# The values' products of two attentions by two query blocks, in float32r parts

## The chip, the cores and the metric

The kernel runs on one core of a Trainium2 chip. The core has a matrix engine (TensorE, PE in the rows; its loading of the stationary operand is PEld), a vector engine (VectorE, DVE), an engine for functions of one operand (ScalarE, ACT), a general one (GpSimd, POOL) and one that starts transfers (SyncE, SP). Each works through its own queue in order, and waits for the others by semaphores. Products land in PSUM, which has banks of 128 x 512 float32; only VectorE and ScalarE read them out in this kernel. The metric is the time of one execution in microseconds on the device.

## The reference

Two transformer layers over 1024 tokens of 1024 features, all in float32. The change touches one attention of each. In both, a query's weights are taken with the values of the keys up to its own block of 128 queries:

```
# layer 1: stick-breaking attention, 8 heads of 64
z = einsum('bhqd,bhkd->bhqk', q, k) * scale
log_keep = where(mask, log_sigmoid(-z), 0)             # mask: key < query
rest = cumsum(log_keep, reverse=True) - log_keep
a = where(mask, exp(log_sigmoid(z) + rest), 0)
out = einsum('bhqk,bhkd->bhqd', a, v)
# layer 2: latent attention (MLA), 8 heads, keys of 96, values of 64
logits = where(allowed, einsum('bhqd,bhkd->bhqk', q, k) * scale, -1e30)
out = einsum('bhqk,bhkd->bhqd', softmax(logits), v)
```

Beside them stand a gated delta rule, projections and gates in layer 1, and a differential attention, a feed-forward block and a gated embedding in layer 2. They keep their code, but for where they lie beside the two attentions.

## The kernel before

**Parts.** Most products run on operands that are split into two float32r parts, high and low, whose sum is the float32 value: `mm3` makes three products of them (L252 to L254). Weights are split by GpSimd (`W`, L243, L244), what comes out of PSUM by `split_evac`: ScalarE casts the high part out of the bank (L301), and VectorE then subtracts it from the same bank for the low part (L302). The products of weights and values (L907) are the exception: they are plain float32, and such a product is two records in the trace.

**The two attentions.** `sb` (L855 to L878) and `mla` (L1171 to L1220) go through the heads in four pairs, and for each pair through eight query blocks of 128. Blocks 0 to 3 take both heads in one item, blocks 4 to 7 one head per item: 12 items a pair. `s0` makes an item's logits `z` in PSUM (two buffers of two banks) and its weights `e` (in `sb` ScalarE's absolute value, exponential and logarithm, VectorE's scan, and another exponential into `cs`; in `mla` VectorE's maximum, ScalarE's exponential with its sum and GpSimd's scaling). `s1` runs two items behind (`attend`, skew 2) and calls `attend_pv`: for up to four blocks of weights at a time it transposes them on TensorE into one PSUM bank `pt` (L903), has them copied to `aT` (L904: VectorE in `sb`; in `mla` ScalarE for an item's first copy and VectorE for its second), and then multiplies (L907) with the values as the stationary operand, 64 columns wide, and 128 queries moving. One bank `po` gathers two heads of a query block, and VectorE copies it to `ob` (L878, L1220).

**Banks and filling.** `banks(2, 1)` is in force in both stages: two banks for projections (`pj`), one for transposes (`pt`), four for `z`, one for `po`. `mix` puts units of other projections between the yields of an attention: in `sb` the projections of the first layer (`proj_z` among them), in `mla` what is left of `diff_proj`, the differential attention's projection, of which the first part runs beside `mla_proj`. `diff_proj` transposes its queries and keys through the same `pt` bank, and a tile `qb_st` with two buffers goes to DRAM. A scheduler then places each engine's instructions, so that rows of all these stand mixed in the queues.

**Where the values come from.** Three places write them to DRAM, each by a ScalarE copy: `vba` (L494, layer 1's first four heads), `proj_b` (L785, `vt2`), and `k_mm` (L1096, a tile `l_v` of four token tiles, in `mla_proj`). `dr_v` and `dr_mv` hold them in float32, and each attention loads a pair's values in one transfer. In `mla_proj`, `fin` transposes queries and keys (L1124), splits them (`l_st`) and sends them off (L1127).

Of the kernel before, what the change touches and what calls it, by code (L numbers as in the profile page):

```python
# [11 lines left out]
F32 = mybir.dt.float32  # L12
# [10 lines left out]
D = 1024  # L23
# [6 lines left out]
# ---------------------------------------------------------------- host layout  # L30
# [121 lines left out]
class Kern:  # L152
    def __init__(self, ctx, tc, d, out):
        self.tc, self.nc, self.d, self.out = tc, tc.nc, d, out
        self.ctx = ctx
        self.const = ctx.enter_context(self.pool("const"))
# [21 lines left out]

    def banks(self, n, m):
        """from here on n banks for products, m for transposes"""  # L180
# [10 lines left out]
    def consts(self):  # L191
# [19 lines left out]
        # strict causal mask in [query, key] layout: key >= query masked  # L211
# [3 lines left out]
        # keys of the next 64-chunk, hidden from the first half of a query block  # L215
# [40 lines left out]
    def fm(self, w, act, kt, ct, half):  # L256
        """feature-major [128 features, 512 tokens] of weight column tile ct"""
# [6 lines left out]
    def tm(self, w, act, kt, tp, c0=0, n=256):  # L264
        """token-major [128 tokens, 2 token tiles, n features]"""
# [8 lines left out]
    def rsqrt(self, v, n, scale, eps, pool=None):  # L274
        """(v * scale + eps) ** -0.5 of a [128, n] tile, in full float32"""
# [21 lines left out]
    def split_evac(self, hi, lo, ps, scale=None):  # L297
        """hi + lo = ps * scale, both f32r"""
# [18 lines left out]
    def norm_half(self, get, gain, xn, pool, h):  # L317
        """rms norm of 4 token-major tiles, transposed to feature-major f32r pairs"""
# [21 lines left out]
    def norm_in_place(self, x, gain, pool, evac, deep=False):  # L340
        """the same of [128, 4, D] in place, and what evac does with its transposes"""
# [23 lines left out]
    def mix(self, main, fill, end=2.0):  # L365
        """units of fill between those of main; both yield how far they are, and fill is at end when main is done"""
# [7 lines left out]
    # ------------------------------------------------------------ layer 1  # L374
    def layer1(self):
# [3 lines left out]
        self.dr_v = dr("dr_v", [2, NT, 128, 256])  # L379
# [105 lines left out]
    def proj_a(self, wv, w):  # L485
# [3 lines left out]
        def vba(w, t):  # L489
# [6 lines left out]
            nc.sync.dma_start(self.dr_v[0, t], vt)  # L496

        def conv(c, u):
            """causal convolution and silu"""
# [11 lines left out]
        def post(c, s):  # L511
            """token-major keys and values, sums of squares"""
# [47 lines left out]
    def gdr(self):  # L560
# [13 lines left out]
        def chunk(c):  # L574
# [32 lines left out]
            # q and k in place times exp(cumulated decay)  # L607
# [10 lines left out]
            for l in range(5):  # L618
                # rows of the second block of each pair, columns of the first
# [65 lines left out]
            # o * rsqrt(mean(o^2) + EPS * dk * (ssq + EPS))  # L685
# [14 lines left out]
        # two chunks at a time, half a chunk apart  # L700
# [976 lines left out]
```

## Time and profile before

| | us |
|---|---|
| median of 3 runs | 2750.32 |
| lowest and highest run | 2749.12, 2760.20 |
| span of the profiled execution | 2761.4 |
| TensorE busy in it | 2628.9 (95%) |
| VectorE busy | 1454.1 (53%) |
| ScalarE busy | 865.7 (31%) |
| GpSimd busy | 1058.8 (38%) |

The profiled execution lies near the slowest of the three runs. The stick-breaking stage stands at about 558 to 940 us of the span, the latent queries', keys' and values' projection at 1180 to 1440, the latent attention at 1440 to 1650, the differential attention behind it. A duration in a row is an instruction's own, from start to end; TensorE's instructions overlap, so that the distance from one start to the next says what one costs in a stream.

### The profile page before, as it was taken

The page shows a single profiled execution, that of the slowest core. Times are in us where ns is not written, and L with a number is a line of the kernel's source. Part 1 is how long each engine was busy: PE and PEld are TensorE (multiplying, and loading weights), DVE is VectorE, ACT ScalarE, POOL GpSimd, SP SyncE. Part 2 cuts the span into 40 slices and gives each one's busy share as a digit, 9 for nine tenths or more (in the row PEclk, how much of TensorE's full clock was granted, in tenths as well). Part 3 has the DMA queues.
Part 4 walks back from the last instruction along what each step waited for, and adds up shares of the span by engine and source line. Part 5 has one row for each costly group of instructions (what it writes and reads, how often), then busy time and mean ns, then how long its engine had stood idle before and what let it go on. Part 6 is the DMA issues. An engine that isn't in the chain of part 4 may idle for free. (4 is left out here: it accounts for less than half of the span.)

```text
span 2761.4 us, 38977 instructions
## 1 busy us (share of the span) xinstructions
PE 2628.9 (95%) x15298; PEld 2201.4 (80%) x15298; DVE 1454.1 (53%) x2837; ACT 865.7 (31%) x1575; POOL 1058.8 (38%) x920
## 2 busy tenths in 40 slices
PE   6998999999999999999889999999999999999999
PEld 6888888877777778989777786779777777777789
DVE  6665555275666554457844334765544454534372
ACT  3322222153344332122324333563433333201031
POOL 2433332212122234544533231223577777633322
PEclk9999999999999999999999996999999999999999
DMA  4423223242321355322673336444212222433222
GB/s 152 136 99 108 69 85 100 74 117 82 106 68 64 111 193 182 115 78 83 207 200 119 98 121 164 136 147 167 65 63 91 78 65 89 164 110 101 75 81 89
DMA packets 150031, 307.27 MB, mean 111 GB/s; under 512 B 13876, under 2 KB 57140, under 8 KB 149848
## 3 DMA queue, kind: packets, MB, share of 16 engines
q1 hardware_dynamic: 149848, 304.78, 35.2%
q8 instruction: 121, 1.98, 0.3%
q14 instruction: 62, 0.51, 0.1%
HBM read 207.72 MB, written 99.37 MB: 111 GB/s over the span
## 5 line engine op out<-in xcount | busy, mean ns | idle before, releaser
L243 POOL TENSOR_SCALAR hl<-raw 128x512 fp32r<-128x512 f32 (+3 forms) x270 | 198.3, 739 | 968.9 <-PE pj L254 958.2
L244 POOL TENSOR_TENSOR hl<-raw,hl 128x512 fp32r<-128x512 f32 (+3 forms) x270 | 368.9, 1372 | 16.2
L252 PE MATMUL pj<-hl,xn_0h 128*128 128x256 f32 (+2 forms) x544 | 161.3, 297 | 2.4 <-DVE qb_raw L730 1.2
L253 PE MATMUL pj<-hl,xn_0h 128*128 128x256 f32 (+2 forms) x544 | 161.1, 296 | 1.7 <-POOL hl L244 1.7
L252 PE MATMUL pj<-hl,xn_1h 128*128 128x256 f32 (+2 forms) x544 | 159.4, 293 | 0.0
L254 PE MATMUL pj<-hl,xn_1l 128*128 128x256 f32 (+2 forms) x544 | 159.4, 293 | 0.0
L254 PE MATMUL pj<-hl,xn_0l 128*128 128x256 f32 (+2 forms) x544 | 159.3, 293 | 0.0
L253 PE MATMUL pj<-hl,xn_1h 128*128 128x256 f32 (+2 forms) x544 | 158.9, 292 | 0.0
L1508 POOL TENSOR_TENSOR hl<-w_s,hl 128x512 fp32r<-128x512 f32 x88 | 121.5, 1382 | 84.1 <-ACT hl L1507 84.0
L907 PE MATMUL po<-aT,v 128*64 128x128 f32 x1152 | 150.1, 280 | 0.8 <-DVE ob L1220 0.5
L252 PE MATMUL pj<-hl,f_hh 128*128 128x512 f32 x352 | 139.8, 397 | 5.0 <-DVE xres L1618 2.8
L254 PE MATMUL pj<-hl,f_hl 128*128 128x512 f32 x352 | 140.4, 401 | 2.9 <-DVE f_hl L1609 2.9
L907 PEld LDWEIGHTS po<-aT,v 128*64 128x64 f32 x1152 | 116.5, 136 | 29.3 <-issue 21.0
L253 PE MATMUL pj<-hl,f_hh 128*128 128x512 f32 x352 | 138.3, 393 | 0.0
L904 DVE COPY aT<-pt 128x512 f32<-128x512 f32 (+3 forms) x128 | 72.6, 567 | 120.2 <-PE pt L903 120.1
L1618 DVE TENSOR_TENSOR xres<-xres,pj 128x512 f32<-128x512 f32 x96 | 65.1, 685 | 127.6 <-PE pj L254 114.6
L1508 POOL TENSOR_TENSOR hl<-raw,hl 128x512 fp32r<-128x512 f32 x66 | 100.1, 1522 | 71.6 <-ACT hl L1507 70.9
L1563 DVE TENSOR_TENSOR f_u<-pj,w_u 128x512 f32<-128x512 f32 x44 | 30.4, 692 | 170.4 <-ACT w_u L1531 96.3
L252 PE MATMUL pj<-xn_0h,hl 128*128 128x512 f32 x288 | 116.9, 406 | 0.0
L252 PE MATMUL pj<-xn_1h,hl 128*128 128x512 f32 x288 | 115.9, 403 | 0.0
L254 PE MATMUL pj<-xn_0h,hl 128*128 128x512 f32 x288 | 114.8, 399 | 0.0
L254 PE MATMUL pj<-xn_1h,hl 128*128 128x512 f32 x288 | 114.6, 398 | 0.0
(599 smaller groups left out, 7505.3 us busy)
## 6 DMA issues: line engine op xcount, KB each, us to landing
raw<-in_w_o_dram SPq DMA_DIRECT2D x28, 512.0 KB, 4.3
dr_mla<-l_st SPq DMA_DIRECT2D x32, 384.0 KB, 4.0
qk<-dr_mla SPq DMA_DIRECT2D x32, 384.0 KB, 4.9
raw<-in_w_fg_dram SPq DMA_DIRECT2D x22, 512.0 KB, 4.5
raw<-in_w_fu_dram SPq DMA_DIRECT2D x22, 512.0 KB, 3.5
dr_h<-f_y SPq DMA_DIRECT2D x22, 512.0 KB, 5.3
raw<-in_w_fd_dram SPq DMA_DIRECT2D x22, 512.0 KB, 4.0
f_y<-dr_h SPq DMA_DIRECT2D x22, 512.0 KB, 4.4
```

Of the source, the lines that this page charges most:

```text
L243: nc.gpsimd.tensor_scalar(hl[:, 0], raw[:, k:k + c], 1.0, 1.0, ALU.mult, ALU.mult)
L244: nc.gpsimd.tensor_tensor(hl[:, 1], raw[:, k:k + c], hl[:, 0].bitcast(F32), ALU.subtract)
L252: mm(ps, lh[0], rh[0], start=first, stop=False)
L253: mm(ps, lh[0], rh[1], start=False, stop=False)
L254: mm(ps, lh[1], rh[0], start=False, stop=last)
L904: copy[b0 > 0](aT[:, b0:b0 + len(bs), :], pt[:, :len(bs), :])
L907: mm(po[64 * h:64 * h + 64, :], v[:, j, h * 64:h * 64 + 64], aT[:, b, :], start=j == 0, stop=j == i)
L1508: nc.gpsimd.tensor_tensor(hl[:, 1], v, hl[:, 0].bitcast(F32), ALU.subtract)
L1563: nc.vector.tensor_tensor(u, ps, v, ALU.add)
L1618: nc.vector.tensor_tensor(xr, xr, ps, ALU.add)
```

## The change

- **Values in two parts.** The three places write high and low parts by `split_evac` instead of a copy. `dr_v` and `dr_mv` double: per head 64 high columns and 64 low ones beside each other. `l_v` now holds two token tiles and is sent twice as often, with one buffer.
- **Two query blocks at a time.** `attend_two` replaces `attend` for both: when the second block of a pair of blocks `u` has its weights and the delay (skew 2 in `sb`, 1 in `mla`, counted in items) has passed, `s1` runs once for both. The new `attend_pv` goes by pairs of key blocks. For each head it transposes four blocks (three in the last pair) into the bank `pt`, and `split_evac` makes two float32r parts of them. Then come the products, for each key block, head and part one: the stationary operand is 128 columns, high and low values, the moving one 256 queries (128 for the last key block). In `po` the first 64 rows gather the high values' share, the others the low values'; `halves` adds them (ScalarE copy, VectorE addition), per head.
- **Counts.** Per attention: 320 float32r products instead of 288 float32 ones (576 records); the same 288 transposes, in 80 fillings of the bank instead of 88; 80 casts and 80 subtractions instead of 88 copies; 16 transfers of `ob` instead of 4 (`sb`) or 8 (`mla`).
- **Buffers.** `e` has 7 instead of 2 and `cs` 4 in `sb` (the scan now runs in place), and 5 instead of 3 in `mla`; `aT` has 3 and 2. `qb_st` has one buffer instead of two in layer 2. The values are loaded by halves, the second half later, and `mla` loads its queries and keys in another order.

```diff
@@ vba
-            vt = cv.tile([128, 256], F32, tag="vt", name="vt")
-            nc.scalar.copy(vt, ps[:, :256])
+            vt = cv.tile([128, 4, 2, 64], F32R, tag="vt", name="vt")
+            self.split_evac(vt[:, :, 0], vt[:, :, 1], ps[:, :256].rearrange("p (h f) -> p h f", h=4))
...
@@ qk_stack
-                st = pool.tile([128, 2, 512], F32R, tag="qb_st", name="qb_st", bufs=2)
+                st = pool.tile([128, 2, 512], F32R, tag="qb_st", name="qb_st", bufs=1 + (pool is not self.fp))
...
@@ sb
-            e = new("e", 2)
+            e = new("e", 7)
...
-            cs = new("cs", 4)
+            cs = e
...
@@ k_mm, in the loop over four token tiles
-                nc.scalar.copy(vt[:, j], pv[:, :, 1, :])
+                if j % 2 == 0:
+                    vt = lp.tile([128, 2, 4, 2, 64], F32R, tag="l_v", name="l_v", bufs=1)
+                self.split_evac(vt[:, j % 2, :, 0], vt[:, j % 2, :, 1], pv[:, :, 1, :])
...
@@ mla
-            e = sp.tile([128, 1024], F32, tag="e", name="e", bufs=3)[:, :len(hs) * nk].rearrange("p (a k) -> p a k", a=len(hs))
+            e = sp.tile([128, 1024], F32, tag="e", name="e", bufs=5)[:, :len(hs) * nk].rearrange("p (a k) -> p a k", a=len(hs))
...
-        def s1(p, i, hs):
...
+        def s1(p, u):
             qks, v = st[p]
...
+            po = po_.tile([128, 2, 256], F32, tag="po", name="po")
+            yield from self.attend_pv(sp, po, self.weights(st, p, u), v, u, 2)
+            ob = sp.tile([128, 256], F32, tag="ob", name="ob", bufs=1)
+            self.halves(ob, po)
+            nc.sync.dma_start(self.dr_mix[:, p, u * 256:(u + 1) * 256], ob)
...
+        yield from self.attend_two(s0, s1, 1)
@@ attend_pv
+        for jp in range(u + 1):
+            slots = [(j, a) for j in (2 * jp, 2 * jp + 1) for a in range(2) if j <= 2 * u + a]
+            aT = []
+            for h in range(2):
+                pt = self.PT()
+                for b, (j, a) in enumerate(slots):
+                    nc.tensor.transpose(pt[:, b, :], e[a, h][:, j * 128:j * 128 + 128], self.ident)
+                n = len(slots)
+                hl = sp.tile([128, 2, 4, 128], F32R, tag="aT", name="aT", bufs=bufs)
+                self.split_evac(hl[:, 0, :n], hl[:, 1, :n], pt[:, :n])
+                aT.append(hl)
+            for j in (2 * jp, 2 * jp + 1):
+                b = [n for n, s in enumerate(slots) if s[0] == j]
+                q = slice((2 - len(b)) * 128, 256)
+                for h in range(2):
+                    for n in range(2):
+                        nc.tensor.matmul(po[:, h, q], v[j // 4][:, j % 4, h], aT[h][:, n, b[0]:b[-1] + 1],
+                                         start=j + n + h == 0, stop=j == 2 * u + 1 and n + h == 2, skip_group_check=True)
+            yield
+    def halves(self, ob, po):
+        for h in range(2):
+            R = slice(64 * h, 64 * h + 64)
+            self.nc.scalar.copy(ob[R], po[0:64, h])
+            self.nc.vector.tensor_tensor(ob[R], ob[R], po[64:128, h], ALU.add)
```

The change also moves instructions. In the queues below `pt`, `aT`, `po`, `z` and `pj` are the tiles named above, `hl` a weight's part, `xn_1h` and `mix00h` operands of projections; what stands in brackets are the engines' semaphores that the row waits for. L936 and L946 are the changed kernel's transposes and products, L255 its third line of `mm3`, L954 `halves`.

TensorE in the stick-breaking stage before, one item's transposes and part of its products:

```order
L903 MATMUL pt<-cst,cs 128x128 [waits PE_49,Activation_49]
L903 MATMUL pt<-cst,cs 128x128 x3
L252 MATMUL pj<-xn_0h,hl 128x512 [waits Pool_49]
L253 MATMUL pj<-xn_0l,hl 128x512
L254 MATMUL pj<-xn_0h,hl 128x512 [waits Pool_49]
L252 MATMUL pj<-xn_0h,hl 128x512
L907 MATMUL po<-aT,v 64x128 [waits DVE_49]
L907 MATMUL po<-aT,v 64x128 x3
```

and in the same stage of the changed kernel, one pair of key blocks, from the second head's transposes on:

```order
L936 MATMUL pt<-cst,e 128x128 [waits DVE_49]
L936 MATMUL pt<-cst,e 128x128 x3
L946 MATMUL po<-aT,v 128x256
L255 MATMUL pj<-xn_1h,hl 128x512
L253 MATMUL pj<-xn_1h,hl 128x512
L254 MATMUL pj<-xn_1l,hl 128x512
L946 MATMUL po<-aT,v 128x256 [waits Activation_49]
L255 MATMUL pj<-xn_1h,hl 128x512
L253 MATMUL pj<-xn_1h,hl 128x512
L254 MATMUL pj<-xn_1l,hl 128x512
L255 MATMUL pj<-xn_1h,hl 128x512
L253 MATMUL pj<-xn_1h,hl 128x512
```

In both a projection's rows stand between the transposes and the products that need them; the transposes now wait for VectorE, which reads the bank second.

TensorE in the last pair of heads of the latent attention before:

```order
L903 MATMUL pt<-cst,e 128x128 [waits Activation_49]
L903 MATMUL pt<-cst,e 128x128 x2
L907 MATMUL po<-aT,v 64x128 x4
L253 MATMUL pj<-hl,mix00h 128x256
L254 MATMUL pj<-hl,mix00l 128x256
L252 MATMUL pj<-hl,mix01h 128x256
L253 MATMUL pj<-hl,mix01h 128x256
L254 MATMUL pj<-hl,mix01l 128x256
L907 MATMUL po<-aT,v 64x128 [waits DVE_49]
L907 MATMUL po<-aT,v 64x128 x2
```

and in the changed kernel, also in the latent attention behind the filling's last row:

```order
L946 MATMUL po<-aT,v 128x256 [waits DVE_49]
L946 MATMUL po<-aT,v 128x256 x4
L936 MATMUL pt<-cst,e 128x128 [waits PE_49]
L936 MATMUL pt<-cst,e 128x128 x3
L946 MATMUL po<-aT,v 128x256 [waits Activation_49]
L936 MATMUL pt<-cst,e 128x128 [waits DVE_49]
L936 MATMUL pt<-cst,e 128x128 x3
L946 MATMUL po<-aT,v 128x256
L946 MATMUL po<-aT,v 128x256 [waits Activation_49]
L946 MATMUL po<-aT,v 128x256 [waits DVE_49]
L946 MATMUL po<-aT,v 128x256 x4
```

No projection's row is left between them: transposes and products alternate, and five products stand between VectorE's subtraction and the next transposes.

ScalarE near the end of the latent attention before (L1207 the exponentials, L1235 a filling's copy):

```order
L904 COPY aT<-pt 128x512 [waits PE_49,Activation_49] x2
L1207 ACTIVATE e,a_s<-z,a_m 128x896 [waits DVE_49,Pool_49]
L904 COPY aT<-pt 128x512 [waits PE_49,Activation_49]
L1207 ACTIVATE e,a_s<-z,a_m 128x896 [waits DVE_49,Pool_49]
L1207 ACTIVATE e,a_s<-z,a_m 128x1024 [waits DVE_49,Pool_49]
```

and in the changed kernel (L1268 the exponentials, L302 the casts):

```order
L302 CAST aT<-pt 128x512 [waits DVE_49,PE_49,Activation_49]
L302 CAST aT<-pt 128x512 [waits DVE_49,PE_49]
L1268 ACTIVATE e,a_s<-z,a_m 128x896 [waits PE_49,Pool_49]
L302 CAST aT<-pt 128x384 [waits DVE_49,PE_49]
L1268 ACTIVATE e,a_s<-z,a_m 128x1024 [waits Pool_49]
L302 CAST aT<-pt 128x384 [waits DVE_49,PE_49]
L954 COPY ob<-po 64x256 [waits DMAHW2_49,PE_49]
L1268 ACTIVATE e,a_s<-z,a_m 128x1024 [waits DVE_49]
```

An exponential now stands between two casts of one group, and waits for TensorE (the transposes that free its buffer) where it waited for VectorE's maximum.

## Rows read from the trace of the kernel before

**Rows 1.** Busy time of each engine in the two attentions' stretches, with granted clock.

```profile
core 0: us, PE busy (x) PEld busy (x) DVE busy (x) ACT busy (x) POOL busy (x), PEclk, DMA share, GB/s
558.00:940.00 382.00, 380.05 (x1951) 276.33 (x1951) 238.86 (x291) 162.95 (x203) 76.96 (x72) 1.00 0.27 82
1440.00:1650.00 210.00, 207.29 (x1469) 165.72 (x1468) 84.27 (x173) 81.83 (x182) 61.12 (x77) 1.00 0.39 117
```

**Rows 2.** Groups by line and shape, 558 to 940 us: busy, mean ns, idle before.

```profile
L907 PE MATMUL po<-aT,v 128*64 128x128 f32 x572 | 74.8, 280 | 0.3 <-DVE aT L904 0.2
```

**Rows 3.** The same view of 1440 to 1650 us.

```profile
L907 PE MATMUL po<-aT,v 128*64 128x128 f32 x576 | 74.9, 280 | 0.5 <-DVE ob L1220 0.5
...
L1207 ACT ACTIVATION_READ_ACCUMULATOR e<-z,a_m 128x1 f32 x60 | 11.9, 198 | 0.0
...
L1207 ACT ACTIVATE e<-z,a_m 128x1024 f32<-128x1024 f32 x8 | 8.9, 1115 | 5.2 <-DVE a_r L1208 2.4 <-DVE a_m L1204 2.1 <-PE pt L903 0.7
```

**Rows 4.** Timeline of TensorE near 701 us: start, duration, engine, line, operation.

```profile
700.80 0.38 PE L903 MATMUL pt<-cst,cs 128*128 128x128 f32 x2
701.11 1.52 PE L907 MATMUL po<-aT,v 128*64 128x128 f32 x12
702.56 0.50 PE L254 MATMUL pj<-xn_1h,hl 128*128 128x512 f32 x1
702.90 0.39 PE L252 MATMUL pj<-xn_1h,hl 128*128 128x512 f32 x1
703.13 0.40 PE L253 MATMUL pj<-xn_1l,hl 128*128 128x512 f32 x1
```

**Rows 5.** Timeline near 1563 us, in the latent attention.

```profile
1562.76 0.59 ACT L904 COPY aT<-pt 128x512 f32<-128x512 f32 x1 [3.04 <-PE pt L903]
...
1563.39 0.44 PE L903 MATMUL pt<-cst,e 128*128 128x128 f32 x2
...
1563.87 0.42 DVE L904 COPY aT<-pt 128x256 f32<-128x256 f32 x1 [0.83 <-PE pt L903]
```

**Rows 6.** What the transposes (L903) sat idle for, us and times.

```profile
  DVE aT L904: 7.7, 21
  ACT aT L904: 7.6, 28
```

**Rows 7.** Timeline of TensorE near 1570 us.

```profile
1570.29 0.28 PE L252 MATMUL pj<-hl,xn_0h 128*128 128x256 f32 x1
1570.41 0.28 PE L253 MATMUL pj<-hl,xn_0h 128*128 128x256 f32 x1
```

**Rows 8.** Timeline near 1459 us: transposes, cast and subtraction of a query stack.

```profile
1458.21 0.63 PE L747 MATMUL pt<-cst,qb_raw 128*128 128x128 f32 x4
...
1458.88 0.58 ACT L301 CAST qb_st<-pt 128x512 fp32r<-128x512 f32 x1 [1.67 <-PE pt L747]
...
1459.49 0.69 DVE L302 TENSOR_TENSOR qb_st<-pt,qb_st 128x512 fp32r<-128x512 f32 x1
```

**Rows 9.** Busy time of the tiles pj alone (PE, PEld, DVE, ACT), the latent attention.

```profile
1440.00:1650.00 210.00, 37.23 (x253) 31.98 (x252) 0.69 (x1) 3.51 (x6) 1.00 0.39 117
```

**Rows 10.** Busy time by stretch, where the granted clock is low (columns of rows 1).

```profile
1430.00:1440.00 10.00, 6.14 (x29) 5.98 (x30) 1.45 (x4) 3.00 (x9) 1.30 (x4) 0.69 1.08 238
1680.00:1720.00 40.00, 39.72 (x118) 25.80 (x119) 18.78 (x67) 17.09 (x48) 0.00 (x0) 0.50 0.42 119
```

**Rows 11.** Timeline of TensorE, 1433 to 1436 us, the latent attention's first products.

```profile
1433.86 0.45 PE L252 MATMUL z<-qk 96*128 96x128 f32 x1 [4.74 <-DMA qk<-dr_mla]
...
1435.76 0.41 PE L253 MATMUL z<-qk 96*128 96x256 f32 x1
1435.97 0.41 PE L254 MATMUL z<-qk 96*128 96x256 f32 x1
```

**Rows 12.** Busy time in a stretch of the latent projection (columns of rows 1).

```profile
1340.00:1350.00 10.00, 9.38 (x70) 8.50 (x69) 9.87 (x42) 6.66 (x19) 1.92 (x2) 1.00 0.95 306
```

**Rows 13.** The tile l_v: from its transfer's issue to its landing.

```profile
DMA to landing us min/median/max: 2.9/4.2/4.7
```

**Rows 14.** The tile l_st: what its engines sat idle for, us and times.

```profile
  DMA dr_mla<-l_st: 28.6, 17
```

More of the change, by code (lines that the diff above doesn't have):

```diff
@@ L828, in sb, with values @@
         st = {}
+        def values(p, half):
+            v = sp.tile([128, 4, 2, 128], F32R, tag=f"v{half}", name="v", bufs=2 - half)
+            nc.sync.dma_start(v.bitcast(F32).rearrange("p t h f -> p t (h f)"), self.dr_v[p // 2, 4 * half:4 * half + 4, :, 2 * (p % 2):2 * (p % 2) + 2].rearrange("t p h a f -> p t (h a f)"))
+            st[p][1].append(v)
         def first(p):
             qk = [self.load_qk(sp, self.dr_qk[p], 0)]
-            v = sp.tile([128, NT, 128], F32, tag="v", name="v", bufs=2)
-            nc.sync.dma_start(v, self.dr_v[p // 2, :, :, (p % 2) * 128:(p % 2) * 128 + 128].rearrange("t p f -> p t f"))
+            v = []
             st[p] = [qk, v]
+            values(p, 0)
         def s0(p, i, hs):
@@ L840, in s0 @@
                 st[p][0].append(self.load_qk(sp, self.dr_qk[p], 1))
-                st[p].append(sp.tile([128, 1024], F32, tag="ob", name="ob", bufs=1))
+            if i == 2:
+                values(p, 1)
             if i == 4 and hs[0] == 0 and p < 3:
@@ L887, in pairs, with attend_two @@
         return [(p, i, hs) for p in range(4) for i in range(NT) for hs in ([(0, 1)] if i < 4 else [(0,), (1,)])]
-    def attend_pv(self, sp, po_, st, e, v, i, hs, *copy):
-        nc = self.nc
-        mm = nc.tensor.matmul
-        if hs[0] == 0:
-            st["po"] = po_.tile([128, 128], F32, tag="po", name="po")
-        po = st["po"]
-        blocks = [(a, j) for a in range(len(hs)) for j in range(i + 1)]
-        aT = sp.tile([128, 8, 128], F32, tag="aT", name="aT", bufs=2)
-        step = 4 if i != 2 else 3
-        for b0 in range(0, len(blocks), step):
-            pt = self.PT()
-            bs = blocks[b0:b0 + step]
-            for b, (a, j) in enumerate(bs):
-                nc.tensor.transpose(pt[:, b, :], e[:, a, j * 128:j * 128 + 128], self.ident)
-            copy[b0 > 0](aT[:, b0:b0 + len(bs), :], pt[:, :len(bs), :])
-        for b, (a, j) in enumerate(blocks):
-            h = hs[a]
-            mm(po[64 * h:64 * h + 64, :], v[:, j, h * 64:h * 64 + 64], aT[:, b, :], start=j == 0, stop=j == i)
-        return po
+    def attend_two(self, s0, s1, skew):
+        items = self.pairs()
+        size = lambda it: (it[1] + 1) * len(it[2]) + 6
+        total, done = sum(size(it) for it in items), 0
+        for n in range(len(items) + skew):
+            if n < len(items):
+                s0(*items[n])
+                done += size(items[n]) / 2
+                yield done / total
+            if n < skew:
+                continue
+            p, i, hs = items[n - skew]
+            if i % 2 and hs[-1] == 1:
+                u = i // 2
+                part = sum(size(it) for it in items if it[0] == p and it[1] // 2 == u) / 2 / (u + 1)
+                for _ in s1(p, u):
+                    done += part
+                    yield min(1.0, done / total)
@@ new lines, in weights, with attend_pv @@
+    def weights(self, st, p, u):
+        e = {}
+        for a in range(2):
+            i = 2 * u + a
+            for hs in [(0, 1)] if i < 4 else [(0,), (1,)]:
+                w = st.pop((p, i, hs))
+                for k, h in enumerate(hs):
+                    e[a, h] = w[:, k]
+        return e
+    def attend_pv(self, sp, po, e, v, u, bufs):
+        nc = self.nc
+        for jp in range(u + 1):
[17 more added lines that the diff above has]
+            yield
@@ L1168, in load, with values @@
         def load(p, hh, c, half):
-            t = sp.tile([96, 2, 512], F32R, tag=f"qk{c}{half}{hh}", name="qk", bufs=1 + (hh == 1 and c == 1 and half == 0))
+            if c:
+                t = sp.tile([96, 2, 512], F32R, tag=f"k{half}{hh}", name="k", bufs=1 + (hh == 1 and half == 0))
+            else:
+                t = sp.tile([96, 2, 512], F32R, tag="q", name="q", bufs=3)
             nc.sync.dma_start(t.bitcast(F32), self.dr_mla[2 * p + hh][:, 2 * c:2 * c + 2, half * 512:half * 512 + 512])
             st[p][0][hh, c, half] = t
+        def values(p, half):
+            v = sp.tile([128, 4, 2, 128], F32R, tag=f"v{half}", name="v", bufs=1)
+            nc.sync.dma_start(v.bitcast(F32).rearrange("p t h f -> p t (h f)"), self.dr_mv[:, 4 * half:4 * half + 4, 2 * p:2 * p + 2].rearrange("p t h a f -> p t (h a f)"))
+            st[p][1].append(v)
         def first(p):
-            v = sp.tile([128, NT, 128], F32, tag="v", name="v", bufs=2)
+            v = []
             st[p] = {}, v
-            for key in ((1, 1, 0), (0, 0, 0), (1, 0, 0)):
+            for key in ((1, 1, 0), (0, 0, 0)):
                 load(p, *key)
-            nc.sync.dma_start(v, self.dr_mv[:, :, p * 128:p * 128 + 128])
         def s0(p, i, hs):
@@ L1184, in s0 @@
                     first(p)
-                for key in ((0, 1, 0), (0, 1, 1), (0, 0, 1), (1, 1, 1), (1, 0, 1)):
+                for key in ((0, 1, 0), (1, 0, 0), (0, 1, 1), (0, 0, 1), (1, 1, 1)):
                     load(p, *key)
-            if i == 4 and hs[0] == 0 and p < 3:
-                first(p + 1)
+            if i == 1:
+                values(p, 0)
+            if i == 4 and hs[0] == 0:
+                load(p, 1, 0, 1)
+                values(p, 1)
+                if p < 3:
+                    first(p + 1)
             nk = (i + 1) * 128
```

43 lines of the change are left out of this document (17 added, 26 removed).

## The prediction

> **What bounds the kernel now.** I read three views in this order: the busy time by stretch, the groups of instructions by line and shape, and the timeline of single products. The change touches two stages of attention and three places where values are written, so each is read by its own stretch. In the stick-breaking stage TensorE is busy for 380.05 of 382 us and in the latent stage for 207.29 of 210, at full clock in both; VectorE has 239 and 84 us there, ScalarE 163 and 82 [rows 1]. So both stages are bounded by TensorE's own work, and the next engine has room. The values' product itself is 572 and 576 records of 74.8 and 74.9 us busy [rows 2, 3], but those durations overlap. In the timeline twelve records (six products, a float32 product being two records) go from 701.11 to 702.56: 0.121 us a record. The float32r product behind them takes 0.34 us to the next one, where the one after takes 0.23: leaving float32 costs 0.11 [rows 4].
>
> The other thing to see is the one PSUM bank for transposes. Before, a single reader empties it: a copy begins at 1562.76, lasts 0.59, and the next transposes begin at 1563.39 [rows 5]. With 0.6 of transposes ahead that is about 1.3 us for each filling. TensorE waits for that in only 7.7 + 7.6 us of the whole program [rows 6], because other products stand in its queue.
>
> **Stick-breaking stage, TensorE.** Removed: 576 records x 0.121 = 70 us, and 48 exits (one for each item of the stage, 4 pairs x 12) x 0.11 = 5. Added: 320 float32r products for 288 float32 ones, 256 of them 256 columns wide. Such a product begins 0.12 us after the one ahead of it [rows 7], 256 x 0.12 = 31. The 64 of 128 columns are not in the trace in this form; they cost no more than a 256-column one and no less than half of it, 64 x 0.06 to 0.12 = 4 to 8, and I take the lower, since a stream shrinks with its columns here (0.23 for 512, 0.12 for 256). So TensorE gets 75 - 35 = 40 us less.
>
> **The bank gets two readers.** Now ScalarE casts the high part out of the bank and VectorE subtracts from the same bank behind it, and only then may the next transposes write it. The kernel has this pattern already in another step: four transposes at 1458.21, cast at 1458.88 for 0.58, subtraction at 1459.49 for 0.69, bank free at 1460.18 [rows 8]. That is 1.97, with a signal 2.03 us a filling against 1.3. There are 80 fillings per attention instead of 88. In the order, the five products that wait for VectorE's subtraction stand ahead of the next transposes once per pair of key blocks, 5 x 0.12 = 0.6, 40 times. The chain is 80 x 2.03 + 40 x 0.6 = 186 us. In the stick-breaking stage TensorE still has 380 - 40 = 340 us, and the projection's rows stand between the transposes and the products in the order, so the chain is covered. What isn't: the casts queue behind the absolute value, exponential and logarithm on ScalarE, the subtractions behind the scan on VectorE. The nearest row is the 7.7 us by VectorE's copies [rows 6]; times 2.03 / 1.3 it is 12, 4 more; the far end is that 40 of the 80 fillings wait for the whole subtraction, 40 x 0.69 = 28. I take 7, near the row. **Term: -33 us (-44 to -12; the low end has no wait and 4 us for entries into float32 that I don't count).** The output's evacuation becomes four operations instead of two per two blocks; the next block's transposes and cast (1.25 us) run meanwhile, so I cost it at nothing; with that cover gone it is at most 0.6 + 0.69 a block, 16 blocks, 20 us.
>
> **Latent stage.** Here the filling work, another attention's projection, ends early in the new order: its last row stands in the third group of the second pair of heads, and from there some 2.4 of the 4 pairs have nothing but their own work. TensorE's own work for a pair was about 43 us (207 less the filling's 37 [rows 9], over 4) and falls by 10 to 33. The chain of a pair is 20 x 2.03 = 41, less 8 x 0.3 where a filling has three blocks (an estimate: 0.125 of transposes and some 0.1 each of cast and subtraction), plus 10 x 0.6: 44 us. Moreover the weights' five buffers come free by the last transposes of a group, so about five exponentials a pair wait for them and then stand ahead of the next cast in ScalarE's queue: 1.115 + 0.198 us each [rows 3], 6.6. So 51 us a pair, more than the 33 of TensorE: the bank becomes the bound. 2.4 x 51 = 122; the 1.6 pairs with filling have a chain of 82 and TensorE's work of 1.6 x 33 + 37 = 90, of which I take the greater. 122 + 90 = 212 against 207; where the chain's waits and the filling meet I count nothing more. **Term: +5 us.** The bounds: no exponential in the way, -6.6 x 4 = -26, or each twice, +16 on the tail; since both ends are extreme I keep -20 to +18.
>
> **Clock.** In that tail TensorE would be busy 33 of 51 us, 65%. Where it was busy for 6.14 of 10 us the granted clock was 0.69, but a single gap lasted 4.74 us there; at the start of the next attention it is 0.50 for 40 us [rows 10, 11]. At the lower level (1.2 GHz) the 256-column product follows after 0.21 us instead of 0.12 [rows 7, 11]. If the whole tail ran at that level, each filling's four transposes would cost 0.5 more (four take 0.63 us and two 0.38 [rows 4, 8], so 0.125 each at full clock) and each five products 0.6 more: 20 x 0.5 + 10 x 0.6 = 16 a pair, 38 in all. Full clock costs 0. Gaps in the tail are about 1 us each, which no row of this kernel shows for long, so I take the middle, **+19 (0 to +38)**. On this the Trainium skill, page "TensorE: Matmul & The Clock Gate", speaks both ways: in "Loop structure matters more than you think" an evacuation by VectorE does not end the warm state, by which the term is 0 and the whole sum -20 instead of -1; in "A second HAM failure mode: psum-queue depth-cycling" frequent small idles between groups let the clock swing, by which it is up to +38 and the sum +18. No row here has such a tail, so neither decides.
>
> **Writing the values.** The latent values become 16 casts and 16 subtractions for 16 copies. A 256-wide VectorE evacuation takes 0.42 us [rows 5], so 16 x 0.42 = 7 us are added to VectorE, which is busy for 9.87 of 10 us in that stretch [rows 12], with TensorE at 9.38: partly on the path. The tile for them holds two token tiles instead of four and has one buffer, so seven casts wait for a landing of 4.2 us [rows 13], and behind such a cast stand on ScalarE the casts of the latent queries and keys, which already sit 28.6 us waiting for their own landings [rows 14]. The stack of the other attention's queries and keys, filling work here, loses its second buffer, so that each of its casts waits for a landing as well; its wait stands in the upper bound. Nothing is bound below zero here, since work is only added. All seven landings exposed would be 7 x 4.2 = 29, but the next tile's projection and VectorE's work lie between; I take a quarter, 2 more of the subtractions' 7 hidden: **+8 (+2 to +20).** The first layer's 8 and 4 subtractions stand among work that TensorE covers (0 to 1), and the values' transfers double with time to spare, their consumers being hundreds of us later.
>
> **Sum.** -33 + 5 + 19 + 8 = -1 us. The profiled span, 2761.4 us, stands 0.4% above the median of the runs, 2750.3, near the run of 2760.2; taken off the median the sum gives 2749 us.
>
> **The rivals.**
> - *The chain is bound, but the clock holds and the landings are covered.* -33 + 5 + 2 = -26: 2724. For it: the gaps are about 1 us, and the landings have work around them. Against it: the 0.69 and 0.50 above.
> - *TensorE stays the bound in the latent stage too*, because the fillings overlap better than the order shows. 40 us in each attention: -80, 2670. Against it: a filling cannot begin before the subtraction ends, 80 x 2.03 = 162 us already, and the filling work is gone after 1.6 pairs. It needs a fill in under 1.6 us.
> - *Slower: TensorE at the lower level through the latent tail.* -33 + 5 + 38 + 8 = +18, and +31 with the exponentials at their upper bound; about 2774. It decides from a tail (last filling row to the last values' product) longer than some 160 us at a granted clock near 0.5; below 140 us it doesn't hold.
> - *The change doesn't do what it says:* float32r products of this shape cost as much as the float32 ones. The 256-column row speaks against it (0.12); TensorE would gain nothing and the waits would remain, 7 + 19 + 8 = 34: 2784. I give it no chance of its own but count it in the slower cases.
>
> **How the numbers follow.** A measurement of this kernel can tell some 0.5%, 14 us, from no change: 2737 to 2764. My forecast, chain and clock each at their middle, has 0.42; the rival with full clock 0.25; TensorE bound 0.05; the lower clock 0.28. So faster 0.30, same 0.42, slower 0.28; the time is that of the forecast, 2749. The range runs from -44 (stick-breaking at -44, latent 0, no clock loss) to +42 (stick-breaking at -12, latent +5, clock +38, values +11): 2706 to 2792; it leaves out the case of -80 and the ends where all terms agree. The forecast's own range is 2730 to 2764.
>
> **What would show it.** The stick-breaking stage should take about 349 us instead of 382, TensorE still over 95% busy. The products of line 946 should follow each other at 0.12 us within a group of four. In the latent stage the transposes of line 936 should mostly have sat idle until VectorE's subtraction, of the order of 0.7 us at some 50 fillings; TensorE about 65% busy in its second half; and the granted clock there says which rival holds: 1.00 the faster one, 0.5 the slower. If the two stages shorten alike, the bank's chain was priced wrong; if the stick-breaking stage is not 20 us shorter, the waits on ScalarE and VectorE were; if the stretch before the latent stage grows by more than 20 us, the landings were.

## The result

The changed kernel takes 2792.8 us (2788.8 to 2794.2) against 2755.3 us for the kernel before (four runs; it was 2750.3 with the three ahead of the prediction): a ratio of 1.0138, 95% interval 1.0117 to 1.0158. It is slower by 38 us; the forecast was 2749 with a range up to 2792. The profiled execution of after has a span of 2786.6 us, 25 more than that of before, since before's span, 2761.4, lies above its kernel's median time and after's below. The differences by stretch below therefore add up to 25 and not to 38. A stretch in a single profile is also uncertain by some us: the stick-breaking attention begins at 546.8 us in after and at 550.7 and 551.3 in two of the runs below that have the same code ahead of it.

The head of its profile page, busy time and share of the span:

```profile
span 2786.6 us, 38328 instructions
...
PE 2586.3 (93%) x14786; PEld 2169.8 (78%) x14786; DVE 1508.9 (54%) x2897; ACT 942.0 (34%) x1751; POOL 1065.7 (38%) x920
```

TensorE is busy for 43 us less than before and the kernel takes longer: what the products gave back was spent waiting. Where, the busy time by stretch shows (first span and length, then each engine, granted clock, DMA). After:

```profile
540.00:925.00 385.00, 366.47 (x1754) 268.13 (x1752) 247.57 (x288) 213.02 (x320) 91.26 (x80) 0.98 0.33 97
1416.00:1661.00 245.00, 209.29 (x1233) 169.48 (x1233) 117.19 (x210) 108.46 (x249) 62.28 (x80) 0.88 0.37 112
1511.00:1661.00 150.00, 116.83 (x578) 89.23 (x578) 67.83 (x122) 61.88 (x140) 31.44 (x40) 0.80 0.28 89
1661.00:1680.00 19.00, 0.77 (x4) 0.61 (x4) 1.89 (x7) 0.93 (x3) 0.00 (x0) 0.50 0.75 205
```

and the two stretches of before that answer to the second and the last row:

```profile
1434.00:1650.00 216.00, 213.29 (x1496) 171.53 (x1497) 85.72 (x177) 84.83 (x191) 62.42 (x80) 0.98 0.41 120
1650.00:1671.00 21.00, 19.34 (x161) 18.93 (x161) 6.25 (x14) 1.34 (x3) 12.53 (x14) 1.00 0.74 217
```

- **Stick-breaking attention** (first row; [rows 1]): from its first logits to its last values' product 390 us before and 381 after, and TensorE is no longer busy all the time.
- **Latent attention**: 216 us became 245. Behind the last row of filling work (1511 us) TensorE is busy for 117 of 150 us, at a granted clock of 0.80.
- **Between the latent and the differential attention** TensorE was busy for 19.3 of 21 us before; after, for 0.8 of 19.
- **Behind it**: the differential attention's code is the same, but its first products start 8 us later than before and its last ones 26 us later.

The waits behind the latent attention, in the changed kernel (who waited for whom: us, times, longest):

```profile
PE z L1361 <- DMA q<-dr_dqk: 18.2, 1, 18.2
```

and the loads of the mixers' output (tile `m_o`) for the first part of the output product, before and after:

```profile
L1365 SPq DMA_DIRECT2D m_o<-dr_mix x8: 319/346/450, 1618.0 to 1734.5; - x8
```

```profile
L1423 SPq DMA_DIRECT2D m_o<-dr_mix x6: 319/322/326, 1679.6 to 1710.4; - x6
```

In both kernels the differential attention's loads start only behind the latent one's last products (I put it down to its tiles, which must come free; no run tests that), so some 20 us go by. Before, `m_o` had been loaded from 1618.0 us on. Of 192 products of that output (256 columns, 0.12 us each [rows 7], 23 us) 35 stood in the latent attention and 157 in the gap behind it. After, `m_o` comes at 1679.6, behind the other loads, and the 192 products stand inside the differential attention. The forecast had no term for this.

### The profile page after: what moved, and what is told of

Read it like the earlier page. It is cut to its first block, busy times and chain, and to the rows that moved or that the text cites. A ratio compares the mean times of both kernels' runs of the same rounds, so it can differ in the third digit from the quotient of the medians.

```text
span 2786.6 us, 38328 instructions
## 1 busy us (share of the span) xinstructions
PE 2586.3 (93%) x14786; PEld 2169.8 (78%) x14786; DVE 1508.9 (54%) x2897; ACT 942.0 (34%) x1751; POOL 1065.7 (38%) x920
## 5 line engine op out<-in xcount | busy, mean ns | idle before, releaser
L244 POOL TENSOR_SCALAR hl<-raw 128x512 fp32r<-128x512 f32 (+3 forms) x270 | 207.0, 772 | 1028.5 <-PE pj L255 1017.5
L946 PE MATMUL po<-aT,v 128*128 128x256 f32 (+1 forms) x640 | 159.3, 334 | 28.1 <-ACT aT L302 20.6
L303 DVE TENSOR_TENSOR aT<-pt,aT 128x512 fp32r<-128x512 f32 (+1 forms) x160 | 101.4, 634 | 135.1 <-ACT aT L302 133.5
L946 PEld LDWEIGHTS po<-aT,v 128*128 128x128 f32 x640 | 109.3, 208 | 69.2 <-ACT aT L302 48.0
L255 PE MATMUL pj<-hl,xn_0l 128*128 128x256 f32 (+2 forms) x544 | 160.8, 296 | 0.0
L255 PE MATMUL pj<-hl,xn_1l 128*128 128x256 f32 (+2 forms) x544 | 156.9, 288 | 0.0
L255 PE MATMUL pj<-hl,f_hl 128*128 128x512 f32 x352 | 140.4, 401 | 2.9 <-DVE f_hl L1667 2.8
L302 ACT CAST aT<-pt 128x512 fp32r<-128x512 f32 (+1 forms) x160 | 86.6, 541 | 154.5 <-PE pt L936 153.1
L253 PE MATMUL pj<-xn_1h,hl 128*128 128x512 f32 x288 | 115.7, 402 | 0.0
L255 PE MATMUL pj<-xn_0h,hl 128*128 128x512 f32 x288 | 115.5, 401 | 0.0
```

Of the source, the lines that this page charges most:

```text
L244: nc.gpsimd.tensor_scalar(hl[:, 0], raw[:, k:k + c], 1.0, 1.0, ALU.mult, ALU.mult)
L253: mm(ps, lh[0], rh[0], start=first, stop=False)
L255: mm(ps, lh[1], rh[0], start=False, stop=last)
L302: nc.scalar.copy(hi, ps)
L303: nc.vector.tensor_tensor(lo, ps, hi.bitcast(F32), ALU.subtract)
L946: nc.tensor.matmul(po[:, h, q], v[j // 4][:, j % 4, h], aT[h][:, n, b[0]:b[-1] + 1], start=j + n + h == 0, stop=j == 2 * u + 1 and n + h = ...
```

## The experiments

Two causes were to be told apart: the one bank for transposes with its two readers (with the clock that falls while TensorE waits), and the place of the output product's units. A third question was why the stick-breaking attention gained so little. Ratios are to the kernel before, in runs on the same chip.

**Each attention alone.** The edit is to take the other's functions from the kernel before.

> The change in the stick-breaking attention alone (values of layer 1 in two parts, two query blocks at a time there); latent attention, its values and the query stack's two buffers as before. Theory 1: the loss lies in the latent attention and behind it, so this half keeps the 7 us that the profile of after shows for its stretch: 2755 - 7 = 2748 us, ratio about 0.997. Theory 2, that the two readers of the bank hurt in both attentions: 2760 or more. The prediction's own term would give 2755 - 33 = 2722.

> The change in the latent attention alone; stick-breaking attention and layer 1's values as before. Theory 1: from the end of the first attention on the profile of after loses 25.6 + 11.5 = 37 us against before, so 2755 + 37 = 2792 us, ratio 1.013, with the output product's first units behind the start of the differential attention as in after. Theory 2: half of the loss, 2773.

Measured: the stick-breaking half 0.9958 (0.9941 to 0.9975), 2744.4 us, 12 us faster. The latent half 1.0166 (1.0144 to 1.0188), 2801.1 us, 46 us slower by the ratio, 9 more than the first theory gave. Together 34, near the 38 of the whole change. So all of the loss comes with the latent attention, and the other half is worth a third of what was forecast for it.

**The output product's place.** SBUF, the memory for tiles, gives a possible reason why `m_o` comes late. By the sizes of its tiles the latent attention's pool grew from 66 to 69 KB (per partition), two more buffers of weights being part of it, and by a map of all tiles it then reaches into the bytes of the two buffers of `m_o`, which it had not touched before. (The map is a working from the kernel; no trace shows addresses.) Two runs test it from both sides. In the first the changed kernel gives up 16 KB below `m_o`:

```diff
-                x = self.xp.tile([128, 4, D], F32, tag="x", name="x", bufs=2)
+                x = self.xp.tile([128, 4, D], F32, tag="x", name="x", bufs=1)
```

In the second the kernel before gets a pool that is 4 KB larger, and for that one buffer less for the query stack, with its products as they were:

```diff
-            e = sp.tile([128, 1024], F32, tag="e", name="e", bufs=3)
+            e = sp.tile([128, 1024], F32, tag="e", name="e", bufs=4)
...
-                st = pool.tile([128, 2, 512], F32R, tag="qb_st", name="qb_st", bufs=2)
+                st = pool.tile([128, 2, 512], F32R, tag="qb_st", name="qb_st", bufs=1 + (pool is not self.fp))
```

> The changed kernel with one buffer instead of two for the residual tile x of the output product's first part, which lies below the tile m_o: so m_o no longer shares addresses with the latent attention's pool. Theory 1 (m_o's loads stand behind the next attention's loads because of the shared addresses, and 192 products that filled TensorE's wait between the two attentions move behind it): the wait of 18 us at the differential attention's start is filled again, 2793 - 17 = 2776 us, ratio to before 1.0075. Theory 2 (the loss is the bank chain and the lower clock alone, the products' place doesn't matter): 2793, as after.

> The kernel before with a fourth buffer for the latent attention's weights and one buffer less for the query stack, which makes room for it: only the pool grows by 4 KB, so that it shares addresses with m_o. Theory 1: m_o's loads move behind the differential attention's, TensorE waits some 18 us there and the 192 products come later: 2755 + 17 = 2772 us, ratio 1.006. Theory 2: no change, 2755.

Measured: 1.0076 (1.0054 to 1.0098), 2776.8 us, and 1.0058 (1.0042 to 1.0075), 2772.5 us. Both are what the first theory gave, to 1 us. In the second the latent attention itself keeps its length (its last logits stand at 1635.3 instead of 1635.6 us), `m_o` is late, and the wait is there:

```profile
L1366 SPq DMA_DIRECT2D m_o<-dr_mix x8: 319/326/1393, 1663.4 to 1745.3; - x8
```

```profile
PE z L1304 <- DMA q<-dr_dqk: 16.9, 1, 16.9
```

In the first, `m_o` is loaded from 1531.3 us on. One thing came out otherwise than I had written: the wait at the next attention's start only fell from 18.2 to 12.0 us, since 143 of the 192 products now ran earlier, inside the latent attention from 1536.8 us on. The gain is the same, because they no longer stand behind.

```profile
L1423 SPq DMA_DIRECT2D m_o<-dr_mix x8: 319/389/458, 1531.3 to 1758.3; - x8
```

```profile
PE z L1361 <- DMA q<-dr_dqk: 12.0, 1, 12.0
```

**The bank.** First without its second reader: the subtraction is left out, so that the weights have no low part and the high part is used twice.

```diff
-                self.split_evac(hl[:, 0, :n], hl[:, 1, :n], pt[:, :n])
+                nc.scalar.copy(hl[:, 0, :n], pt[:, :n])
...
-                        nc.tensor.matmul(po[:, h, q], v[j // 4][:, j % 4, h], aT[h][:, n, b[0]:b[-1] + 1],
+                        nc.tensor.matmul(po[:, h, q], v[j // 4][:, j % 4, h], aT[h][:, 0, b[0]:b[-1] + 1],
```

Then with both readers, but two banks. (The edit holds for more than its label says: these banks also serve the differential attention and the projection `ple_proj` behind it, which so have one bank for projections instead of two.)

```diff
-        with self.banks(2, 1):
+        with self.banks(1, 2):
             self.mix(self.mla(), fill)
```

> The changed kernel without VectorE's subtraction behind the cast in both attentions: the weights' low part is left out, and its products take the high part a second time, so the products' number stays. The bank for transposes then has one reader. Theory 1 (in the latent attention a filling costs 2.0 us because two engines empty the bank in turn, 0.7 of it the subtraction): some 50 fillings without other work, 50 x 0.7 = 35 us less there, and some 10 of the stick-breaking stage's 19 us of idle time: 2793 - 45 = 2748 us. Theory 2 (the exponentials and the clock set the pace): less than 15 us gained, 2780.

> The changed kernel with two banks for transposes and one for projections in the latent attention (two and one in the other order before). Theory 1: the second head's transposes no longer wait for the subtraction of the first, so that a pair of fillings takes about 2.0 + 0.8 instead of 2 x 2.03 us; 25 such pairs without other work, 1.2 us each: 2793 - 30 = 2763 us, less what the filling loses by its single bank. Theory 2 (casts and exponentials on ScalarE's queue are the bound): 2785 to 2795.

Measured: 0.9946 (0.9925 to 0.9966), 2742.8 us, and 1.0030 (1.0015 to 1.0045), 2763.2 us. The edit to two banks takes back 30 us, that to one reader 50. The latent stretch, 245 us in after, is 200 with one reader and 207 with two banks, TensorE busy for 182 and 192 of it and the clock back at 0.96 and 0.97:

```profile
1410.00:1610.00 200.00, 182.26 (x1234) 154.67 (x1234) 69.15 (x132) 108.21 (x251) 62.07 (x80) 0.96 0.47 138
```

```profile
1417.00:1624.00 207.00, 192.47 (x1307) 164.59 (x1307) 116.40 (x211) 108.90 (x251) 62.28 (x80) 0.97 0.46 137
```

So either edit of the bank undoes the loss in this stretch, but the runs don't say how much of it is the waits on the bank themselves: in both, the scheduler also spread the filling work further. Its last row stands at 1565 and 1585 us instead of 1512, so that 43 and 38 us are left without it instead of 150.

The second bank is worth more in its own stretch than 30 us: 38 us there, of which a part is lost again where the projections have one bank. From the differential attention's last products to the next stage's first transposes it is 69 us, against 45 in before and after. After, and then the run with both repairs (further below), which has the same edit, with its longest wait:

```profile
1888.80:1934.00 45.20, 43.66 (x367) 43.31 (x366) 16.65 (x54) 10.75 (x20) 9.54 (x8) 1.00 0.55 205
```

```profile
1845.30:1915.60 70.30, 60.47 (x392) 57.73 (x391) 17.43 (x53) 11.91 (x22) 11.43 (x10) 0.76 0.42 146
PE pj L253 <- ACT p_o L1476: 7.7, 9, 1.6
```

TensorE there waits for ScalarE to empty the one bank (L1476 is `ple_proj`'s copy), and the clock is 0.76 instead of 1.00.

The stick-breaking half of the expectation for one reader did not hold. TensorE's idle time there stayed at 19 us (the stretch became 5 us shorter, 376 for 381), and only its reason changed. After, and then with one reader, in that stretch:

```profile
PE pt L936 <- DVE aT L303: 7.9, 9, 3.3
PE z L862 <- DVE e L876: 5.0, 8, 1.6
```

```profile
PE z L862 <- DVE e L876: 9.5, 11, 2.0
```

With the bank's wait gone, the logits wait longer for their own banks, which VectorE's chain frees (L876 is its last reader of them).

**The clock.** Added products were to keep TensorE busy during the subtraction, in the last two pairs of heads:

```diff
+                if warm:
+                    ps = self.PJ()
+                    for c in range(2):
+                        nc.tensor.matmul(ps[:, :128 * n], v[0][:, 0, 0], hl[:, 0, :n], start=c == 0, stop=c == 1)
```

> The changed kernel with added products whose results nobody reads: for the last two pairs of heads of the latent attention, two products of 512 columns (384 in the last fillings) behind each cast, where TensorE otherwise waits for the subtraction; 80 products, 80 x 0.23 = 18 us of TensorE. Theory 1 (the granted clock of 0.78 in the tail costs some 15 us, and falls because TensorE is idle between the fillings): the clock stays at 1.0 in the last two pairs, and the time falls in spite of the added work, to 2780 or less. Theory 2 (the clock costs nothing, since the waits are for ScalarE and VectorE): 2793 or up to 18 more.

Measured: 1.0253 (1.0231 to 1.0274), 2826.8 us, 34 more than after. This run doesn't answer its question. The scheduler moved the filling work towards the end, beside the added products, and most of the first two pairs stood without it; there the clock fell instead, to 0.71 from 1400 to 1520 us (0.99 in after), and rose to 0.90 in the rest.

```profile
1400.00:1520.00 120.00, 104.85 (x523) 86.24 (x522) 49.29 (x95) 45.02 (x106) 22.34 (x30) 0.71 0.42 124
1520.00:1690.00 170.00, 144.92 (x871) 120.27 (x869) 68.07 (x122) 62.67 (x142) 41.91 (x51) 0.90 0.32 98
```

It shows only that here, too, the low clock lies where the chain stands alone. What it costs has to be read from rows (below).

**The order on TensorE.** In the stick-breaking half alone, the next filling's transposes were written ahead of the products of the pair before; then the same with both repairs.

```diff
+        aT = [fill(0, 0), fill(0, 1)]
         for jp in range(u + 1):
+            nxt = [fill(jp + 1, 0)] if jp < u else []
...
+            if jp < u:
+                nxt.append(fill(jp + 1, 1))
+            aT = nxt
```

> The kernel with the change in the stick-breaking attention alone, where the next filling's transposes are written ahead of the products of the pair of key blocks before (they no longer stand behind the five products that wait for VectorE). Theory 1 (of the 20 us that TensorE idles in that stage about 9 are transposes waiting for the bank): 2744 - 5 = 2739 us. Theory 2 (the waits come from ScalarE's and VectorE's own queues, not from the order on TensorE): 2744 as before.

Measured: 0.9946 (0.9930 to 0.9963), 2739.1 us. The interval overlaps that of the half without this order, so a gain of 5 us isn't shown.

> The changed kernel with both repairs: two banks for transposes in the latent attention (one for projections), and one buffer for the residual tile x, so that m_o shares no addresses with the latent attention's pool. Theory 1 (the two causes are separate and their repairs add up: -30 for the bank, -16 for the order of the transfers): 2793 - 46 = 2747 us, below the kernel before. Theory 2 (with the bank's waits gone there is no room in the latent attention for the output product's units, so the second repair brings nothing more): 2763.

> The same, and the next filling's transposes written ahead of the products in both attentions (with three buffers of transposed weights, for which the latent keys' first tile has one buffer instead of two). Theory 1 (the five products between the subtraction and the next transposes, 0.6 us each time, still stand in the chain): 20 to 25 such places without other work in the latent attention, some 12 us less than with the two repairs alone, 2735 us. Theory 2 (with two banks the other bank's filling covers them): the same as the two repairs, 2747.

Measured: 0.9971 (0.9948 to 0.9993), 2750.3 us, and 0.9968 (0.9952 to 0.9985), 2746.0 us. The two repairs add up, 2793 - 43, and turn the change into a gain of 0.3%. The further order adds nothing that can be told from it. The best kernels tried that keep all parts are the change in the stick-breaking attention alone, 0.4 to 0.5% faster than before, and the repaired whole can't be told from them. That doesn't make the change worthless in the latent attention: its stretch is 207 us with both repairs, 9 less than before, and the 25 us behind the differential attention are the price of the banks' edit there. With the second bank in force in the latent attention alone some 2750 - 25 = 2725 us could be left, an estimate from these rows that no run tests.

## Why the prediction was wrong

**The steps that failed: there was no term behind the latent attention, and the stick-breaking term was three times too large.** The sum said -1 us and 38 came. Some 21 of the 39 are the stick-breaking attention (below), 16 to 17 the missing term. The sum ended with the last values' product. But the order of before, quoted ahead of the prediction, has `mix00h` rows between the latent attention's products, and the order of after has none. I read that as filling work that ends early, and did not ask where those 192 products went and what they had covered. The two runs on `m_o` put this at 16 to 17 us (by the ratios, 1.0138 less 1.0076, and 1.0058, of 2755 us). It hangs on the list of buffers, which I had read only as memory for the chain: by the map, 3 KB more in one pool were enough.

**The latent attention: the mechanism was right, the size somewhat small.** Forecast: the bank becomes the bound, +5 at full clock and +19 for the clock, 24 together; measured 245 - 216 = 29. The cycle was priced well. Timeline of TensorE in after, one pair of key blocks with nothing else (start, duration, idle before and its reason):

```profile
1525.55 0.60 PE L936 MATMUL pt<-cst,e 128*128 128x128 f32 x4
1526.83 0.38 PE L946 MATMUL po<-aT,v 128*128 128x256 f32 x1 [0.68 <-ACT aT L302]
1527.55 0.66 PE L936 MATMUL pt<-cst,e 128*128 128x128 f32 x4 [0.34 <-DVE aT L303]
1527.96 0.36 PE L946 MATMUL po<-aT,v 128*128 128x256 f32 x1
1528.88 0.39 PE L946 MATMUL po<-aT,v 128*128 128x256 f32 x1 [0.56 <-ACT aT L302]
1529.61 0.86 PE L946 MATMUL po<-aT,v 128*128 128x256 f32 x5 [0.34 <-DVE aT L303]
1530.31 0.27 PE L936 MATMUL pt<-cst,e 128*128 128x128 f32 x1
```

From 1525.55 to 1527.55 the first filling holds the bank, 2.00 us (forecast 2.03, of which 0.06 for a signal came from no row); the second with the five products takes 2.76, to 1530.31: 4.76 for the pair against 4.66. TensorE waits once for the cast and once for the subtraction in each filling. What was too small was probably the rest of a pair of heads, where logits and exponentials stand between the fillings; no run isolates it. In the waits of the last 150 us the casts lead, and the logits wait for the exponentials that free their banks, a wait that I had not listed:

```profile
PE po L946 <- ACT aT L302: 17.9, 27, 1.8
PE z L253 <- ACT e L1268: 5.8, 8, 1.0
PE pt L936 <- DVE aT L303: 3.8, 12, 0.4
PE po L946 <- DVE aT L303: 2.1, 6, 0.3
```

So the sign that I had given, transposes idle for some 0.7 us until the subtraction at some 50 fillings, isn't there: TensorE waits longer for the cast, and it was busy for 78% of the time and not 65%.

**The clock: direction and size about right.** The granted clock is 0.80 over those 150 us; between the levels 1.00 and 0.50 that is 60 us at the lower one, in five stretches, the first from 1531.9 us, right behind the pair shown above. At the lower level a second filling goes from 1646.19 to 1649.94, 3.75 us instead of 2.76:

```profile
1646.19 1.12 PE L936 MATMUL pt<-cst,e 128*128 128x128 f32 x4
1646.96 0.56 PE L946 MATMUL po<-aT,v 128*128 128x256 f32 x1
1647.98 2.16 PE L946 MATMUL po<-aT,v 128*128 128x256 f32 x6 [0.46 <-ACT aT L302]
1649.94 0.41 PE L936 MATMUL pt<-cst,e 128*128 128x128 f32 x1
```

By that, 60 x (1 - 2.76 / 3.75) = 16 us, an estimate from one filling; no run isolates it. The longest wait of TensorE in the tail is 1.8 us, so the clock fell here without a long one. Of the two sections of the Trainium skill's "TensorE: Matmul & The Clock Gate" that the prediction weighed, this trace agrees with "A second HAM failure mode: psum-queue depth-cycling": the clock went down and up among short waits. The remark in "Loop structure matters more than you think", that a copy out of PSUM by VectorE doesn't break the warm state, stands there for a loop whose next products follow at once. Here they waited, and mostly for ScalarE's casts (17.9 us, against 5.9 for the subtractions), so this trace doesn't bear on it.

**The stick-breaking attention: a third of the gain.** Forecast -33 (-44 to -12); measured -12. The chain was mostly covered there, but two terms were mis-sized. First, the products and their transposes. From each start to the next, waits taken off, the trace gives 70.4 us for the values' products before and 52.1 after, 33.4 and 27.9 for the transposes: 24 us less where the forecast had 40. In a run of products 0.12 us holds for 256 columns, but one of 128 columns also takes 0.11, where I had taken 0.06. And a product that stands alone often costs more, here 0.22 us from 601.73 to the next start:

```profile
601.73 0.38 PE L946 MATMUL po<-aT,v 128*128 128x256 f32 x1
601.95 0.39 PE L253 MATMUL pj<-xn_0h,hl 128*128 128x512 f32 x1
602.18 0.39 PE L254 MATMUL pj<-xn_0l,hl 128*128 128x512 f32 x1
```

The scheduler set 90 of the 320 so that a projection's row comes next; the median to its start is 0.20 us, 90 x 0.08 = 7 us. (Behind float32 transposes it is 0.20, between two rows of a projection about half take 0.12 and half 0.22.) Second, TensorE idles 19 us instead of 2, where the forecast allowed 7, and the clock falls for 17 us, in which some 10 us of these products and transposes lie. The row from which the 7 was scaled [rows 6] mixes weight loads with products: TensorE's own wait there was 0.5 us in this stage before, and is 7.9 after. Taking away the subtraction did not shorten the idle time: what is late next is the logits' banks, behind VectorE's work. TensorE's gain was real (388 to 366 us busy over about the same stretch), but a second wait stood close behind the first.

**Writing the values: nothing instead of +8.** (The 8 doesn't come out exactly of the numbers beside it, a quarter of 29 being 7.) From the stick-breaking attention's last product to the first latent logits it is 493 us before and 489 after. But the latent half alone, which has the new writing, has 493, and the stick-breaking half alone, which has the old, 489: the 4 us don't come from it, and its own cost can't be told from zero. The landings were mostly covered: five waits of 4.0 us in all for `l_v`, and the other casts' wait for landings fell from 28.6 us [rows 14] to 15.4. After, the tile `l_v` and then `l_st`, us and times:

```profile
  DMA dr_mv<-l_v: 4.0, 5
```

```profile
  DMA dr_mla<-l_st: 15.4, 13
```

**The rivals.** The slower one named the right stretch, but its own test leaves it open: the tail is 150 us, between the 140 and 160 that I gave, at 0.80 and not near 0.5. Its price of 2774 lacked the products' place and had the stick-breaking term as it was. The faster one fell with that clock. The rival with TensorE as the bound fell: a filling costs 2 us on this bank. That the products cost as much as before fell too (52.1 against 70.4 us). That the range's end, 2792, lies within 1 us of the time is luck: it is reached with the whole tail at the lower clock and +11 for the values, and neither came.

## What to carry to other kernels

When a product gets cheaper, price the buffer that feeds it: one PSUM bank that two engines empty in turn cost 2.0 us a filling here, and hid that only as long as other products stood beside it. In an order, look not only at what stands where you changed something but at what stood there before and has gone: 192 foreign products that covered a wait for loads were worth 16 us. Before growing a pool, see what shares its addresses next; here a few KB decided when another stage's loads could be placed. And when a repair brings less than its stretch gains, look for where else its edit is in force: one bank less for projections cost 25 us two stages on.

## What the hardware showed that I had not expected

TensorE's clock fell to half in the tail with no wait longer than 1.8 us (0.80 granted over 150 us, TensorE busy for 117 of them), where the first of the earlier falls that I had looked at [rows 10] stood behind a gap of 4.74 us [rows 11]. The second of them, at the next attention's start, had no such gap either: its longest wait in the 20 us before was 1.3 us. At half clock a pair's second filling took 3.75 us instead of 2.76, less than double, since the cast and the subtraction in it took 0.58 and 0.69 us at either level. And a float32r product of 128 columns followed the one ahead after 0.11 us, hardly less than one of 256 (0.12).
